# Attention with bias: the last seven head pairs' k and q turned by DMA transposes instead of TensorE

## Chip, cores and metric

One NeuronCore of one Trainium2 chip runs the whole computation in one launch. The metric is the device time of that launch in microseconds (us); the profile's "span" runs from the first to the last instruction of one profiled execution.

## What is computed

Softmax attention with an additive bias that all heads share: 4 x 8 = 32 heads, 1024 positions, head size 64, float32 in and out.

```python
scores = scale * np.matmul(q, k.transpose(0, 1, 3, 2))    # scale = 1/8
scores = scores + bias                                    # (1, 1, 1024, 1024)
attn = np.exp(scores - max) / (np.sum(np.exp(scores - max)) + 1e-8)
return np.matmul(attn, v)
```

## The kernel before

**Tiling.** Heads are taken in 16 pairs (`pr` 0 to 15, even head `t` = 0, odd head `t` = 1). Positions are split as p * 8 + c, with p the partition and c one of 8 chunks. A *slot* is one query chunk of one head: 128 queries against all 1024 keys, 131,072 scores. There are 8 x 32 = 256 slots, in two groups of pairs (9 and 7, `GROUPS`); slots 0 to 143 belong to pairs 0 to 8, slots 144 to 255 to pairs 9 to 15. Every head comes first with three of its chunks, then in the middle of the group with two, then at the end of the group with the other three, so that pair p of the second group is wanted for the first time at slot 144 + 6(p - 9).

**A slot's work.** TensorE fills one of three PSUM places (two banks each) with the scores: 8 matmuls with a chunk of the transposed k as weights and the slot's transposed q as the moving operand (`fill_half`, L277). Bias is added by 8 more matmuls against a scaled identity (L274), but only in a few start slots: afterwards a place is not cleared. The next head's scores come by adding the difference, and for that the operands hold two heads at once. `ko` and `qo` of a pair hold k and q of the even head on partitions 0 to 63 and of the odd head on 64 to 127, the even q negated; `ke` and `qe` hold the even head of this pair and the odd head of the pair before, the odd q negated; `qz` and `qs` hold one head beside zeros for the start slots. Then an exponential turns the place into a bfloat16 tile E: on ScalarE one activation over 1024 columns (`exp`, L291), or, for the slots listed in `PLAN`, on VectorE in five instructions (`d_steps`: `fixed` L308, `frac` L314, `square` L319, `cube` L322, `last` L325), of which only `fixed` reads the place. TensorE multiplies E with v (`av`, L342; v carries a column of ones, so the row sums come along), into banks of up to 7 slots in `ps_x`, which VectorE divides out (`evac`, reciprocal L370 and product L372) and SP's queue stores.

**How k and q come to be.** GpSimd's queue loads them with a cast to bfloat16 into the pool `land`. For pairs 0 to 6 they land as rows, the two heads one behind the other (L156, L168); for pairs 7 to 15 (`BESIDE`) each load is cut in two and lands with the two heads side by side in each chunk (`beside`, L146). TensorE turns a pair's chunk by a transpose into a PSUM tile `px` of the pool `ps_x` (`transposes`, L214), the same two tags that `av` uses. VectorE copies it out to `ko` (L226) or, with the sign, to `qo` (L228). From pair 9 on (`EARLY`) the other arrays are made by copies of half the partitions from SBUF to SBUF on SP's queue (`copy`, L592): `ke` straight from `ko`, and `qe`, `qz`, `qs` from a negated `qo`, which VectorE writes over the landed q (`negate`, L251). k and q arrays stand in a ring of nine tiles (`RING`), so pair p cannot be written before pair p - 9 has been read for the last time. For pairs 3 to 6 VectorE sets landed rows side by side in one tile of the pool `side` (`set_beside`, L245), and TensorE transposes from there. v of pairs 0 to 6 lands as rows and is moved into `vall` by VectorE (L545); v of pairs 7 to 15 (`INPLACE`) lands there directly, in two loads (L187).

**The order.** Every engine executes its own list in the order in which it was written, and so does every DMA queue's issuer. That order comes from a planner that runs while the kernel is built: it keeps a clock for each engine, takes at each step the piece of work that can start first by its own constants (`EXP`, `FILL`, `COPY`, `LATER` and so on), and emits it. Waits on the chip are by semaphores that the framework puts in. Thus the constants set the order alone, and the chip's real durations decide who waits in it. `PLAN` lists the slots that VectorE takes.

## Time and profile before

| what | value |
|---|---|
| median of three runs | 226.95 us (226.21 to 228.2) |
| the profiled execution | 227.0 us, its span 225.2 us |
| granted TensorE clock, mean | 0.998 |
| busy: TensorE / ScalarE / VectorE / GpSimd | 218.0 / 215.1 / 200.9 / 94.4 us |
| slots on ScalarE / VectorE | 230 / 26 |
| DMA packets, of them under 512 B | 92,365, of them 76,256 |

Three engines are busy for nine tenths of the span or more, so shares alone don't say which one sets the end. Busy time of a group merges records that overlap; the mean duration of one instruction is that of its record, and records of consecutive instructions overlap by some tens of nanoseconds, so the distance from start to start is a little shorter. In a row of the timeline the first number is the start in us, the second the length of the merged stretch, and the bracket the idle time before it and who ended it.

### The profile page before, as it was taken

The numbers are of one execution on the slowest core, as the hardware profiler recorded it, in microseconds if no ns is written. First come the engines' busy times: TensorE is split into PE (matmuls) and PEld (weight loads), VectorE is DVE, ScalarE is ACT, GpSimd is POOL, SyncE is SP. The second block draws the span as 40 slices with busy tenths as digits, with TensorE's granted clock in tenths as the row PEclk, the third lists the DMA queues.
The fourth block names the chain that finished last, engine by engine and source line by source line (L and its number), as shares of the span: only waits on it lengthen the run. The fifth ranks groups of instructions, "written<-read, shape, count | busy, mean of one in ns | idle before, by whom it ended". The sixth has DMA issues, their size and how long they took to land.

```text
span 225.2 us, 10472 instructions
## 1 busy us (share of the span) xinstructions
PE 218.0 (97%) x4535; PEld 208.2 (92%) x4535; DVE 200.9 (89%) x311; ACT 215.1 (95%) x235; POOL 94.4 (42%) x160
## 2 busy tenths in 40 slices
PE   7999999999999999999999999999999999999994
PEld 2779989999999999999999999999999999999993
DVE  3587888999999999799999999999999999999853
ACT  3799999999999999999999999999999999999993
POOL 8816577767575875307457475661000000000000
PEclk9999999999999999999999999999999999999999
DMA  5999999999999999498999999989111111112123
GB/s 194 218 204 216 225 211 172 169 202 173 131 129 155 112 142 109 60 209 111 200 165 195 182 141 201 119 107 88 45 44 45 44 44 45 44 37 50 44 60 100
DMA packets 92365, 28.95 MB, mean 129 GB/s; under 512 B 76256, under 2 KB 89056, under 8 KB 92320
## 3 DMA queue, kind: packets, MB, share of 16 engines
q0 software_dynamic: 62880, 14.06, 69.2%
q1 hardware_dynamic: 29008, 13.61, 24.1%
q8 instruction: 35, 0.57, 1.1%
q10 hardware_dynamic: 432, 0.62, 0.9%
q14 instruction: 10, 0.08, 0.1%
HBM read 29.36 MB, written 8.39 MB: 168 GB/s over the span
## 4 chain that ended last, share of the span: by engine, by line
PE 57%; ACT 13%; DMA 11%; DVE 10%; issue 6%; SPq 0%; DVEq 0%; ACTq 0%
PE pl L277 32%; PE po L342 17%; ACT E L291 13%; DMA out_dram<-ob 9%; PE px L214 5%; PE pl L274 2%; DMA dy<-in_q_dram 2%; DVE ob L372 2%; DVE dy L308 1%; DVE df L322 1%; DVE ko L226 1%; DVE df L319 1%; PE px L218 1%; DVE qe L239 1%; DVE qo L228 1%
## 5 line engine op out<-in xcount | busy, mean ns | idle before, releaser
L291 ACT ACTIVATE E<-pl 128x1024 bf16<-128x1024 f32 (+1 forms) x231 | 211.9, 1094 | 2.4 <-PE pl L277 2.2
L342 PE MATMUL po<-vall,E 128*128 128x65 bf16 x1840 | 87.3, 194 | 0.7 <-DVE ob L372 0.4
L277 PE MATMUL pl<-qo,ko 128*128 128x128 bf16 x1024 | 76.1, 219 | 0.6 <-ACT E L291 0.2
L342 PEld LDWEIGHTS <-E 128*128 128x128 bf16 x1840 | 74.3, 98 | 1.6 <-DVE ob L372 0.6
L277 PEld LDWEIGHTS <-ko 128*128 128x128 bf16 x1160 | 69.1, 98 | 2.3 <-issue 0.7
L277 PE MATMUL pl<-qe,ke 128*128 128x128 bf16 x888 | 66.7, 219 | 0.6 <-ACT E L291 0.2
L277 PEld LDWEIGHTS <-ke 128*128 128x128 bf16 x888 | 53.5, 98 | 2.8 <-issue 0.3
L308 DVE TENSOR_SCALAR dy<-pl 128x1024 int32<-128x1024 f32 x26 | 31.7, 1220 | 1.3 <-PE pl L277 0.5
L322 DVE SCALAR_TENSOR_TENSOR df<-de,df 128x1024 f32<-128x1024 f16 x26 | 31.6, 1217 | 0.1
L325 DVE SCALAR_TENSOR_TENSOR de<-dy,df 128x1024 uint16<-128x1024 int32 x26 | 31.6, 1217 | 0.1
L372 DVE TENSOR_TENSOR ob<-po,rs 128x448 f32<-128x448 f32 (+4 forms) x40 | 23.3, 583 | 1.4
L146 POOL DMA_DIRECT2D q<-in_q_dram x18 | 16.0, 891 | 9.6 <-DVE q L251 6.6
L146 POOL DMA_DIRECT2D k<-in_k_dram x18 | 16.0, 890 | 8.2 <-PE px L214 5.5
L187 POOL DMA_DIRECT2D vall<-in_v_dram x18 | 16.3, 907 | 6.9 <-PE po L342 4.8
L314 DVE TENSOR_SCALAR de<-dy 128x1024 f16<-128x1024 uint16 x26 | 19.0, 733 | 0.0
L319 DVE TENSOR_TENSOR df<-de 128x1024 f16<-128x1024 f16 x26 | 17.7, 683 | 0.1
L226 DVE COPY ko<-px 128x1024 bf16<-128x1024 bf16 (+1 forms) x16 | 10.7, 666 | 3.5 <-PE px L218 2.2
L228 DVE TENSOR_SCALAR qo<-px,sgn 128x1024 bf16<-128x1024 bf16 (+2 forms) x18 | 12.3, 686 | 0.5 <-PE px L214 0.2
L370 DVE RECIPROCAL rs<-po 128x7 f32<-128x7 f32 (+5 forms) x41 | 8.0, 194 | 5.0 <-PE po L342 4.4
L516 POOL COPY tick<-vall 1x1 bf16<-1x1 bf16 x14 | 9.0, 643 | 6.1 <-DMA vall<-in_v_dram 5.8
L274 PE MATMUL pl<-ident,braw 128*128 128x128 bf16 x136 | 11.5, 227 | 0.0
L342 PE MATMUL po<-vall,de 128*128 128x65 bf16 x208 | 11.0, 194 | 0.0
(63 smaller groups left out, 141.1 us busy)
## 6 DMA issues: line engine op xcount, KB each, us to landing
out_dram<-ob SPq DMA_DIRECT2D x74, 64.0 KB, 2.9
ke<-ko SPq DMA_DIRECT2D x20, 128.0 KB, 4.7
out_dram<-ob SPq DMA_DIRECT2D x24, 96.0 KB, 3.7
k<-in_k_dram POOLq DMA_DIRECT2D x18, 128.0 KB, 4.8
q<-in_q_dram POOLq DMA_DIRECT2D x18, 128.0 KB, 4.7
vall<-in_v_dram POOLq DMA_DIRECT2D x18, 128.0 KB, 5.1
braw<-in_bias_dram POOLq DMA_DIRECT2D x7, 256.0 KB, 5.4
v<-in_v_dram POOLq DMA_DIRECT2D x7, 256.0 KB, 6.7
```

What stands on the lines that cost most here:

```text
L146: nc.gpsimd.dma_start(out=t[:, :, y, :], in_=(qf, kf)[x][pr][:, y].rearrange("p (c d) -> p c d", d=D))
L187: nc.gpsimd.dma_start(out=vall[:, (2 * pr + t) % VR, :, :D], in_=vf[pr][:, t])
L274: nc.tensor.matmul(to, braw[:, c, :].rearrange("p (kp kc) -> p kc kp", kc=NCH)[:, kc, :], ident8[:], start=i == 0, stop=False, skip_group_ ...
L277: nc.tensor.matmul(to, kk[:, kc, :], qq[:, c, :], start=False, stop=True, skip_group_check=True)
L291: nc.scalar.activation(e[:, i:i + n].rearrange("p b x -> p (b x)"), places[slots[s][0]][:, i:i + n].rearrange("p b x -> p (b x)"), ACTF.Ex ...
L308: w.tensor_scalar(t["y"][:], places[slots[s][0]].rearrange("p b x -> p (b x)"), scale * LOG2E * 65536.0, 128.0 * 65536.0, op0=ALU.mult, op ...
L314: w.tensor_scalar(t["f"], t["lo"], CA / 65536.0, CA * CR, op0=ALU.mult, op1=ALU.add)
L319: w.tensor_tensor(t["s"], t["f"], t["f"], op=ALU.mult)
L322: w.scalar_tensor_tensor(t["w"][:], t["f"], -CC, t["s"], op0=ALU.add, op1=ALU.mult)
L325: w.scalar_tensor_tensor(etile[s].bitcast(U16).rearrange("p c q -> p (c q)"), t["y"][:], 1.0 / 512.0, t["w"][:], op0=ALU.mult, op1=ALU.add)
L342: nc.tensor.matmul(po[:, j + i, :], etile[s][:, kc, :], vall[:, slots[s][2] % VR, kc, :], start=j + i + kc == 0, stop=kc == NCH - 1, skip_ ...
L372: nc.vector.tensor_tensor(ob[:, :n, :], po[:, :n, :D], rs[:, :n, :].to_broadcast([P, n, D]), op=ALU.mult)
```

## The change

For pairs 9 to 15 k and q now land as rows, in one load each. VectorE sets the two heads of k side by side in a tile of the pool `side` (L594), and those of q with the sign in two instructions (L597). SP's queue then issues a DMA transpose from that tile straight into `ko` or `qo` (`turn_over`, L570): 14 transposes of 128 x 1024 bfloat16, 256 KB each, which replace 112 transposes on TensorE and 14 copies out of PSUM on VectorE. The negation of `qo` and the copies on SP's queue stay; the negated q is written over the side tile. `next_turn` lets at most four side tiles be held (`SIDES`), a k tile until its transpose has landed, a q tile until the last copy from it has. To make room `land` has three tiles of each name instead of four, and one `qz` serves both groups of pairs. `INPLACE` shrinks with `BESIDE`, so that v of pairs 9 to 15 lands as rows and is moved by VectorE (L548). VectorE gets 27 slots instead of 26, at other places. The seven numbers of `DUE` change too, but they time TensorE transposes of pairs 9 to 15, of which there are none left.

```diff
-    LANDS = 4
+    LANDS = 3
-    SIDE, SIDES, SIDEND = 3, 1, 9
+    SIDE, SIDES, SIDEND = 3, 4, 9
-    qz = [consts.tile([P, NCH, P], BF, name=f"qz{x}") for x in range(2)]
+    qz = consts.tile([P, NCH, P], BF)
-    PLAN = (34, 42, 55, 63, 74, 80, 84, 99, 107, 112, 122, 125, 137, 141, 157, 164, 174, 178, 179, 196, 200,
-            208, 219, 225, 229, 243)
+    PLAN = (34, 42, 57, 60, 67, 83, 89, 93, 96, 110, 115, 134, 141, 145, 151, 155, 171, 178, 187, 193, 198,
+            204, 206, 222, 232, 237, 243)
-    BESIDE = {0: range(7, NP), 1: range(7, NP)}
-    INPLACE = range(7, NP)
+    BESIDE = {0: range(7, 9), 1: range(7, 9)}
+    INPLACE = range(7, 9)
+    XBAR = range(9, NP)
...
-        nc.gpsimd.memset(qz[0][D:, :, :], 0.0)
+        nc.gpsimd.memset(qz[D:, :, :], 0.0)
-        nc.vector.memset(qz[1][D:, :, :], 0.0)
...
+        xbar = [x[:2] for x in pieces if x[0] in XBAR]
+        pieces = [x for x in pieces if x[0] not in XBAR]
...
+        TURN, TURNED, SIDED, held = 7200, 2200, (640, 430), {}
...
+        def turn_over(pr, which, t):
+            nonlocal t_sp, t_dma
+            name = ("qo", "ko")[which]
+            nc.sync.dma_start(out=arrays(pr)[name][:], in_=raws[pr, which, 0].rearrange("p c t d -> p (c t d)"),
+                              transpose=True)
+            t_sp += 850
+            t_dma = max(t_dma, t) + TURNED
+            done = t + TURN
+            ready[("ko", pr) if which else ("qo", pr, 0)] = done
+            if which:
+                held[pr, 1] = done
+            doubles(pr, which, 0, NCH, done, False)
+
+        def next_turn():
+            while xbar and sum(x > t_dve for x in held.values()) < SIDES:
+                pr, which = xbar[0]
+                ring = max(last_slot.get(pr - RING, -1), last_of.get(2 * (pr + 1 - RING), -1) if linked(pr) else -1)
+                r = raw_at.get((pr, which, 0))
+                if r is None or ring >= next_fill:
+                    return
+                xbar.pop(0)
+                held[pr, which] = 1e12
+                cost = SIDED[which]
+
+                def run(t, pr=pr, which=which, cost=cost):
+                    x = side.tile([P, NCH, 2, D], BF, name="side")
+                    if which:
+                        nc.vector.tensor_copy(x.rearrange("p c t d -> p t c d"), lands[pr, which, 0][:])
+                    else:
+                        for i, sign in ((0, -1.0), (1, 1.0)):
+                            nc.vector.tensor_scalar(x[:, :, i], lands[pr, which, 0][:, i], sign, 1.0, op0=ALU.mult,
+                                                    op1=ALU.mult)
+                        freed(pr, t)
+                    raws[pr, which, 0] = x
+                    sp_q.append((t + cost + L_DVE, lambda t3: turn_over(pr, which, t3)))
+                dve_q.append((r, 2, cost, run))
...
-                freed(pr, ready[key])
+                if pr in XBAR:
+                    held[pr, 0] = ready[key]
+                else:
+                    freed(pr, ready[key])
```

How the lists of the engines change, at two places. First VectorE where pairs 9 and 10 are prepared, after the last slot of pair 0 has been read (`px` is the PSUM tile of a TensorE transpose, `ob` a finished bank of outputs, `dy`, `df` and `de` the tiles of the five-step exponential, `side` a side tile, `k16` and `q16` landed rows). Before, these twelve rows stand in a row:

```order
L226 COPY ko_2523<-px_2502 128x1024
L308 TENSOR_SCALAR dy_2544<-pl0_109 128x1024
L228 TENSOR_SCALAR qo_2568<-px_2547,sgn_98 128x1024
L251 TENSOR_SCALAR q16_894<-qo_2568 128x1024
L314 TENSOR_SCALAR de_2597<-dy_2544 128x1024
L319 TENSOR_TENSOR df_2620<-de_2597 128x1024
L226 COPY ko_2652<-px_2622 128x1024
L370 RECIPROCAL rs_2672<-po_2474 128x7
L372 TENSOR_TENSOR ob_2674<-po_2474,rs_2672 128x448
L308 TENSOR_SCALAR dy_2698<-pl2_111 128x1024
L228 TENSOR_SCALAR qo_2730<-px_2710,sgn_98 128x1024
L251 TENSOR_SCALAR q16_1056<-qo_2730 128x1024
```

There the negation (L251) stands right behind the copy that it reads. Now the side tiles of pair 9's k and q are set at this point, those of pair 10 four rows later, and the negations come further on in VectorE's list, behind other work; from pair 9's q (`side_2504`) to its negation:

```order
L597 TENSOR_SCALAR side_2504<-q16_1043 128x8x64 x2
L315 TENSOR_SCALAR de_2531<-dy_2401 128x1024
L315 TENSOR_SCALAR de_2561<-dy_2448 128x1024
L320 TENSOR_TENSOR df_2573<-de_2531 128x1024
L594 COPY side_2593<-k16_1170 128x2x8x64
L597 TENSOR_SCALAR side_2613<-q16_1173 128x8x64 x2
L371 RECIPROCAL rs_2643<-po_2468 128x7
L373 TENSOR_TENSOR ob_2645<-po_2468,rs_2643 128x448
L320 TENSOR_TENSOR df_2663<-de_2561 128x1024
L323 SCALAR_TENSOR_TENSOR df_2573<-de_2531,df_2573 128x1024
L371 RECIPROCAL rs_2725<-po_2622 128x6
L373 TENSOR_TENSOR ob_2727<-po_2622,rs_2725 128x384
```

Behind these twelve come `cube` of another slot and one `fixed`, then pair 9's negation, pair 11's side tiles, another `fixed` and pair 10's negation:

```order
L323 SCALAR_TENSOR_TENSOR df_2663<-de_2561,df_2663 128x1024
L309 TENSOR_SCALAR dy_2786<-pl2_110 128x1024
L252 TENSOR_SCALAR side_2504<-qo_2591 128x1024
L594 COPY side_2820<-k16_1322 128x2x8x64
L371 RECIPROCAL rs_2833<-po_2715 128x6
L373 TENSOR_TENSOR ob_2835<-po_2715,rs_2833 128x384
L597 TENSOR_SCALAR side_2858<-q16_1325 128x8x64 x2
L309 TENSOR_SCALAR dy_2886<-pl1_109 128x1024
L252 TENSOR_SCALAR side_2613<-qo_2675 128x1024
```

So the copies out of PSUM are gone, and VectorE reaches a negation, which reads what a DMA transpose has written, after about ten other instructions. Second, SP's queue at the same place of the program. Before, the stores of one bank are followed by pair 9's copies and the first of pair 10's:

```order
L592 DMA ke_1330<-ko_2523 64x1024
L592 DMA ke_2556<-ko_2523 64x1024
L592 DMA qe_1399<-q16_894 64x1024
L592 DMA qe_2618<-q16_894 64x1024
L592 DMA qz1_102<-q16_894 64x1024
L592 DMA ke_2556<-ko_2652 64x1024
L592 DMA ke_2685<-ko_2652 64x1024
```

Now four transposes and the stores of two more banks go ahead of them:

```order
L570 DMA_TRANSPOSE ko_2543<-side_2499 128x8x128
L570 DMA_TRANSPOSE qo_2591<-side_2504 128x8x128
L570 DMA_TRANSPOSE ko_2631<-side_2593 128x8x128
L570 DMA_TRANSPOSE qo_2675<-side_2613 128x8x128
L810 DMA out_0_dram<-ob_2645 128x2x64
L810 DMA out_0_dram<-ob_2645 128x128
L810 DMA out_0_dram<-ob_2645 128x2x64
L810 DMA out_0_dram<-ob_2645 128x64
L810 DMA out_0_dram<-ob_2727 128x2x64 x2
L810 DMA out_0_dram<-ob_2727 128x64 x2
L632 DMA ke_1310<-ko_2543 64x1024
L632 DMA ke_2818<-ko_2543 64x1024
```

The copies moved behind the transposes and behind eight stores. The last pair's last copy (`qe` of pair 15) stood in SP's list behind the stores of the bank that completes 131 slots and now stands behind those of the bank that completes 159; in TensorE's list 149 slots have been filled before that bank's products, and now 168, while pair 15 is first read when 179 and now 178 have been. TensorE's list itself loses the 112 transposes, and in it the products with v follow the fills more closely: at slot 136 the fills are 17 slots ahead of the products before, and 4 now.

More of the change, by code (lines that the diff above doesn't have):

```diff
@@ L201, in arrays @@
             if pr in first_pair:
-                t["qz"] = qz[group_of[pr] % 2]
+                t["qz"] = qz
             arrs[pr] = t
@@ L451 @@
         pieces += [y for x in zip(k_items[n1:], q_items[n1 + SPLIT:]) for y in x]
+        xbar = [x[:2] for x in pieces if x[0] in XBAR]
+        pieces = [x for x in pieces if x[0] not in XBAR]
         due = {p: d for p, d in zip(range(EARLY, NP), DUE)}
         need_at = {}
-        for p, which, c0, n in pieces:
+        for p, which, c0, n in pieces + [(*x, 0, NCH) for x in xbar]:
             need_at[p, which, c0] = min(s for s, x in enumerate(slots) if x[2] // 2 == p and (c0 == 0 or x[1] >= c0))
@@ L632, in next_side @@
         def next_side():
-            if side_q and len(side_open) < SIDES and side_q[0] in raw_at:
+            if side_q and len(side_open) < 1 and side_q[0] in raw_at:
                 pr, which, c0 = side_q.pop(0)
@@ L859 @@
         while next_fill < NS or next_act < len(acts) or avq or dav or dve_q or sp_q:
+            next_turn()
             c = []
```

2 lines of the change are left out of this document (1 added, 1 removed).

## Prediction

> **What bounds the kernel now.** I read the page first, for the shares, and then ScalarE's timeline, because three engines are nearly full and only a timeline tells which of them never waits.
>
> ```profile
> span 225.2 us, 10472 instructions
> PE 218.0 (97%) x4535; PEld 208.2 (92%) x4535; DVE 200.9 (89%) x311; ACT 215.1 (95%) x235; POOL 94.4 (42%) x160
> ```
> ```profile
> 9.06 31.14 ACT L291 ACTIVATE E<-pl 128x512 bf16<-128x512 f32 x34 [0.47 <-PE pl L277]
> 40.70 18.44 ACT L291 ACTIVATE E<-pl 128x1024 bf16<-128x1024 f32 x20 [0.50 <-PE pl L277]
> 59.38 67.31 ACT L291 ACTIVATE E<-pl 128x1024 bf16<-128x1024 f32 x73 [0.24 <-PE pl L277]
> 126.99 94.58 ACT L291 ACTIVATE E<-pl 128x1024 bf16<-128x1024 f32 x103 [0.30 <-PE pl L277]
> 222.06 0.34 ACTq L767 DMA_DIRECT2D out_dram<-ob  x1
> ```
>
> The reader is to see four stretches of exponentials without a gap, one after the other, from 9.06 to 126.99 + 94.58 = 221.57 us, with 0.47 + 0.50 + 0.24 + 0.30 = 1.5 us of idle time before them, all ended by TensorE's fills. In the last stretch one exponential takes 94.58 / 103 = 0.918 us. At that price the other three should last 33 x 0.918 + 0.6 (one of the 34 is half a slot) = 30.9, 18.4 and 67.0 us; they last 31.14, 18.44 and 67.31, so 0.6 us more of waiting hides in them. ScalarE's list of 230 slots is therefore the bound, about 2.1 us of it are waits, and the rest of the 225.2 us is about 8 us ahead of the first exponential and 3.6 us behind the last. TensorE, busier by the page, waits for ScalarE as often as the other way round; what it is relieved of shows only in those 2.1 us.
>
> The profiled execution took 227.0 us, 1.8 more than its span and within 0.05 of the median of 226.95, so I work from 227.0 and need no correction.
>
> **The change, part by part.** The prices on VectorE and TensorE:
>
> ```profile
> L308 DVE TENSOR_SCALAR dy<-pl 128x1024 int32<-128x1024 f32 x26 | 31.7, 1220 | 1.3 <-PE pl L277 0.5 <-ACT E L291 0.4
> L325 DVE SCALAR_TENSOR_TENSOR de<-dy,df 128x1024 uint16<-128x1024 int32 x26 | 31.6, 1217 | 0.1
> L322 DVE SCALAR_TENSOR_TENSOR df<-de,df 128x1024 f32<-128x1024 f16 x26 | 31.6, 1217 | 0.1
> L314 DVE TENSOR_SCALAR de<-dy 128x1024 f16<-128x1024 uint16 x26 | 19.0, 733 | 0.0
> L319 DVE TENSOR_TENSOR df<-de 128x1024 f16<-128x1024 f16 x26 | 17.7, 683 | 0.1
> L372 DVE TENSOR_TENSOR ob<-po,rs 128x448 f32<-128x448 f32 x27 | 16.9, 624 | 0.9
> L370 DVE RECIPROCAL rs<-po 128x7 f32<-128x7 f32 x27 | 5.4, 200 | 2.0 <-PE po L342 1.8
> L228 DVE TENSOR_SCALAR qo<-px,sgn 128x1024 bf16<-128x1024 bf16 x14 | 10.4, 746 | 0.4 <-PE px L214 0.2
> L226 DVE COPY ko<-px 128x1024 bf16<-128x1024 bf16 x15 | 10.2, 682 | 3.4 <-PE px L218 2.2 <-PE px L214 1.2
> L239 DVE TENSOR_SCALAR qe<-qo 64x384 bf16<-64x384 bf16 x3 | 1.1, 350 | 0.0
> L251 DVE TENSOR_SCALAR q<-qo 128x1024 bf16<-128x1024 bf16 x7 | 3.7, 533 | 0.6
> L545 DVE COPY vall<-v 128x1024 bf16<-128x1024 bf16 x7 | 3.3, 471 | 0.1
> L245 DVE COPY side<-q 128x1024 bf16<-128x1024 bf16 x4 | 2.4, 594 | 3.2 <-PE px L214 3.2
> L245 DVE COPY side<-k 128x1024 bf16<-128x1024 bf16 x4 | 1.7, 431 | 0.3 <-PE px L214 0.3
> ```
> ```profile
> 92.37 0.45 PE px L214 x8
> ```
> ```profile
> 20.00:210.00 190.00, 188.08 (x4010) 183.65 (x4008) 180.48 (x264) 188.81 (x206) 81.53 (x136) 1.00 1.00 125
> 92.00:156.00 64.00, 63.60 (x1371) 62.51 (x1369) 61.07 (x86) 63.58 (x70) 34.56 (x51) 1.00 1.25 155
> ```
>
> *One slot more on VectorE.* ScalarE runs 229 slots instead of 230: -0.92 us on the path that sets the end.
>
> *112 TensorE transposes less.* The chain of waits prices eight of them at 0.45 us, so 14 x 0.45 = 6.3 us of TensorE go, all between about 92 and 140 us, where it is busy for 63.6 of 64. This doesn't shorten ScalarE's list; it can remove ScalarE's waits in that part, the 0.30 at 126.99 and the 0.3 hidden in the stretch before. The waits earlier than 59 us, 1.5 of the 2.1, stay, since loads and lists are the same there but for one fill of zeros that VectorE drops. I take half of the 0.6: -0.3, with 0 and -0.6 as ends.
>
> *VectorE's load.* Gone are 7 x 0.682 + 7 x 0.746 = 10.0 us of copies out of PSUM. Added are 7 side tiles of k at 0.43 to 0.59 (I take 0.43, the row of the same operand), 7 of q as two half-size multiplications (nearest row 0.35 for 384 columns; 0.35 to 0.5 each, I take 0.35, so 4.9 in all), 7 moves of v at 0.47, and one slot of 1.220 + 1.217 + 1.217 + 0.733 + 0.683 = 5.07. That is 3.0 + 4.9 + 3.3 + 5.1 = 16.3, net +6.3 us by records (up to 9.5 with the upper ends). Between 20 and 210 us VectorE is idle for 190 - 180.5 = 9.5 us, so it still fits beneath ScalarE, but with 3 us left, or nothing. In itself this costs 0; without that cover the excess would appear as late `fixed` steps, each of which holds one of three places.
>
> *The DMA transposes.* Nothing in the trace is a transpose. The nearest rows:
>
> ```profile
> ke<-ko SPq DMA_DIRECT2D x20, 128.0 KB, 4.7
> qe<-q SPq DMA_DIRECT2D x13, 128.0 KB, 4.2
> k<-in_k_dram POOLq DMA_DIRECT2D x6, 256.0 KB, 6.9
> ```
> ```profile
> 94.99 1.12 SPq L592 DMA_DIRECT2D ke<-ko  x2
> 128.64 3.04 SPq L767 DMA_DIRECT2D out_dram<-ob  x3
> 138.34 0.47 SPq L592 DMA_DIRECT2D qe<-q  x1
> ```
>
> From 4.2 (a copy of half the bytes) to 9.4 us (two copies of 4.7 end to end); I take 6.9, the row with the same bytes. What hides it is VectorE's list: between pair 9's side tile of q and its negation stand two `frac`, two `square`, two `cube`, one `fixed`, two side tiles and two evacuations: 2 x 0.733 + 2 x 0.683 + 2 x 1.217 + 1.220 + 1.13 + 2 x 0.82 = 9.3 us by records. Starts follow each other more closely than records last, by some 7% (an estimate: over 92 to 160 us the groups' busy times add up to 70 us where VectorE as a whole was busy for 65), so 8.6 us. The transpose is issued behind that of k, 0.56 us later by the copies' row, and would land at 0.56 + 6.9 = 7.5: hidden, with 1 us to spare. At 9.4 VectorE would wait about 1.4 us. For pair 10's q, the fourth transpose of a burst, the list from pair 9's side tile of k to that negation holds 0.7 + 9.3 + 0.533 + 0.43 + 0.82 + 0.7 + 1.220 = 13.7 us by records, 12.7 from start to start; if the four pass one behind the other, they may take (12.7 - 0.56) / 4 = 3.0 us each. Cost by the value taken: 0; by the upper end, see the second rival.
>
> *SP's queue and the wait it adds.* Copies cost SP 0.56 us each, stores up to 3.04 / 3 = 1.0. Fourteen issues at 0.56 to 1.0 are 8 to 14 us more between 92 and 156 us. What is queued behind a transpose are stores and the copies that make `ke` and `qe`; who waits for these is TensorE's fill of the next pair. Pair 15's last copy was issued at 138.34 and is wanted at slot 180, the 161st of ScalarE's list before, whose exponential starts at about 126.99 + 34 x 0.918 = 158 us, its fill 2 us earlier: 17 us of cover. In the new lists that copy stands ten fills ahead of the first use, some 8 us, less 4.2 for its landing. The cover shrinks to about 4 us and is not used up. Cost 0.
>
> *Loads.* k, q and v of seven pairs come in one load each instead of two; GpSimd issues 21 fewer. Three landing tiles instead of four start pair 12's load only when pair 9's q has been set aside, and in VectorE's list those rows are read after the 13 us up to pair 10's negation and 4 more (two `last`, a `frac`, an evacuation), against 6.9 for the landing. The one `qz` left is free once slot 92 is filled, and pair 9's copy into it stands behind the stores of 97 finished slots. Cost 0.
>
> Sum: 227.0 - 0.92 - 0.3 = 225.8 us. Ends: -0.6 from the waits and 0 to +2 for a VectorE with nothing left give 225.5 to 228.
>
> The Trainium skill's page "DMA: Bandwidth & Descriptors", section "Latency and other measured facts", gives DMA transposes an effective 261 GB/s; 256 KB would then pass in about 1.0 us, an estimate, and the forecast would hold with room. The page "VectorE: DVE Perf Modes", section "The three transpose paths", speaks against the change: 1309 ns for 128 x 128 by DMA against 390 by TensorE; eight such blocks one after the other would be 10.5 us, an estimate, and the sum would be that of the third rival. No run here has shown either yet.
>
> **The rivals.** *Everything goes:* also the early waits vanish, 227.0 - 0.92 - 2.1 = 224.0. Against it: three quarters of them lie where nothing changes. Chance 0.08.
>
> *VectorE stands at the negations.* If a transpose lands in 9.4 us instead of 6.9, each of seven negations holds VectorE for about 1.4 us, and behind it wait side tiles, evacuations and `fixed` steps: 10 us, of which 3 are idle anyway, 7 to make up. A single wait is under the 2 x 0.918 us that two other filled places give ScalarE; the sum isn't. If between half and all of the 7 us reach the end, 227.0 - 0.9 + 3.5 to 7 = 229.6 to 233, the middle 231.4. It decides from about 8 us of landing, or 3.0 us each in a burst of four. For it: DMA rows of this stretch are slow, VectorE is full, and four transposes come at once. Against: 6.9 us for the same bytes out of DRAM. Chance 0.27.
>
> *Transposes one after another.* If each holds the stream for its whole 6.9 us, 14 take 97 us, from 92 to 189; with the copies the last pair is there at about 194 instead of 156, and the fixed order makes ScalarE wait for it: 227 - 0.9 + 38 = 264. It decides from (156 - 5 - 92) / 14 = 4.2 us each. For it: nothing in the trace shows how such a transfer spreads over the 16 engines. Against: the copies beside it do overlap, two issued 0.56 us apart landing 4 us after issue. Chance 0.10.
>
> **How the numbers follow.** Forecast 0.55, the three rivals 0.08, 0.27 and 0.10. One per cent, 2.3 us, is about what a measurement of this kernel can tell from no change. Faster by over 1% (under 224.7) is the first rival and the very edge of the forecast: 0.09. Slower by over 1% (over 229.2) are the second and third, 0.37, less a little of the second that stays below: 0.36. Within 1%: 0.55. The forecast's own range is 224.9 to 228. For eight times in ten I leave out the third rival and a few hundredths at either end: 224.4 to 233.
>
> **What would show it.** Right: ScalarE's timeline has 229 slots in gapless stretches from 92 us on, transposes land within 7 us, negations (L252) show no idle time before them. Second rival: VectorE's idle time before L252 or L597, ended by a transpose, about 1.4 us each, and ScalarE idle behind `fixed`. Third: TensorE waiting for `ko`, `ke` or `qe` past slot 144. If VectorE's list simply runs late without any DMA wait, my load sum was too low. The prediction is wrong if transposes cost SP's queue much more than a copy, or if loads through three landing tiles come late.

## The result, and the profile after

The changed kernel takes 246.22 us, the median of four executions (245.59 to 247.23), beside 226.76 us for the kernel before (four, 226.21 to 228.2): 1.084 times as long, with an interval of 1.081 to 1.088. The prediction was 225.8 us and its range ended at 233.0; the time lies 13 us above that end. The profiled execution after took 245.59 us, 18.6 more than the one before (227.0).

The head of the page after, its busy line and three rows of its 40 slices (6.1 us each):

```profile
span 243.6 us, 10179 instructions
PE 218.7 (90%) x4423; PEld 207.8 (85%) x4423; DVE 201.4 (83%) x331; ACT 215.3 (88%) x234; POOL 62.2 (26%) x118
...
DVE  2497899879999999866257688399989999899994
ACT  3699999989999999999821699869999999999993
PEclk9999999999999999999977799979999999999999
```

Hardly an engine has more work than before: ScalarE is busy for 215.3 us (215.1 before), VectorE for 201.4 (200.9), TensorE for 218.7 (218.0). The 18.6 us are waits, all but a fraction, and the slices show where: ScalarE's row falls to 2, 1 and 6 at slices 20 to 22, which is 122 to 140 us, and once more to 6 near 160; VectorE's row thins out earlier, from slice 16 on. ScalarE's timeline has the size of the gaps (start, length, operation, and in brackets the idle time before it and who ended it):

```profile
117.84 2.85 ACT L292 ACTIVATE E<-pl 128x1024 bf16<-128x1024 f32 x3
125.86 1.02 ACT L292 ACTIVATE E<-pl 128x1024 bf16<-128x1024 f32 x1 [5.17 <-PE pl L278]
...
134.53 1.02 ACT L292 ACTIVATE E<-pl 128x1024 bf16<-128x1024 f32 x1 [5.44 <-PE pl L278]
...
138.20 19.36 ACT L292 ACTIVATE E<-pl 128x1024 bf16<-128x1024 f32 x21 [1.36 <-PE pl L278]
160.64 3.77 ACT L292 ACTIVATE E<-pl 128x1024 bf16<-128x1024 f32 x4 [3.08 <-PE pl L278]
```

Four gaps, 5.17 + 5.44 + 1.36 + 3.08 = 15.05 us, all ended by a fill of TensorE's. In all, ScalarE waits 19.5 us for fills, where it was 2.2. From 164.75 us on the exponentials run as densely as before. Three of the four can be followed back row by row. TensorE's two long waits behind the first two, from its timeline:

```profile
118.80 0.61 PE L278 MATMUL pl<-qe,ke 128*128 128x128 bf16 x8
124.29 0.62 PE L343 MATMUL po<-vall,E 128*128 128x65 bf16 x8 [4.88 <-DVE ob L373]
124.72 1.04 PE L278 MATMUL pl<-qo,ko 128*128 128x128 bf16 x8
...
132.96 0.62 PE L343 MATMUL po<-vall,de 128*128 128x65 bf16 x8 [4.93 <-DVE de L326]
```

It waits first for an evacuation (`ob`, L373), then for a `last` step (`de`, L326), both VectorE's. VectorE, from its timeline, had stood before them:

```profile
106.61 0.43 DVE L252 TENSOR_SCALAR side<-qo 128x1024 bf16<-128x1024 bf16 x1 [2.19 <-DMA qo<-side]
...
111.78 0.43 DVE L252 TENSOR_SCALAR side<-qo 128x1024 bf16<-128x1024 bf16 x1 [1.99 <-DMA qo<-side]
...
120.59 0.43 DVE L594 COPY side<-k 128x1024 bf16<-128x1024 bf16 x1 [4.74 <-DMA qz<-side]
...
123.61 0.62 DVE L373 TENSOR_TENSOR ob<-po,rs 128x448 f32<-128x448 f32 x1
...
128.70 0.43 DVE L252 TENSOR_SCALAR side<-qo 128x1024 bf16<-128x1024 bf16 x1 [2.63 <-DMA qo<-side]
```

The negations (L252) wait for a transposed q, 10.7 us in four waits over the whole run. The longest single wait is another one: at 120.59 the side tile of a later k (L594) needs one of the four side tiles, and the one that it gets is free only when the copy into `qz` has landed. The evacuation that TensorE wants from 119.4 us on stands three microseconds of work behind it on the same in-order engine. The gap near 160 us has the same shape: a negation at 155.91 waited 3.92 us for a turned q, TensorE then waited 3.02 us for a `last` step behind it, and ScalarE 3.08 us for TensorE. SP's queue shows why that copy is late; a row is one issue or several of a kind, its second number the time that they hold the queue:

```profile
96.51 1.33 SPq L570 DMA_TRANSPOSE ko<-side  x1
97.95 3.29 SPq L570 DMA_TRANSPOSE qo<-side  x1
101.34 1.62 SPq L570 DMA_TRANSPOSE ko<-side  x1
103.08 3.12 SPq L570 DMA_TRANSPOSE qo<-side  x1
106.31 5.81 SPq L810 DMA_DIRECT2D out_dram<-ob  x8
112.16 1.13 SPq L632 DMA_DIRECT2D ke<-ko  x2
...
114.62 0.60 SPq L632 DMA_DIRECT2D qz<-side  x1
```

The four transposes of pairs 9 and 10 hold the queue from 96.51 to 106.2. Eight stores that had come due meanwhile go next, and pair 9's copies follow at 112.16, though its turned k had landed at 103.1 and its negation was done at 107.0. The `qz` copy, issued at 114.62, has landed when VectorE goes on at 120.59. The view of line 570 gives all fourteen transposes (ns: least, median, most, for which one holds the queue):

```profile
L570 SPq DMA_TRANSPOSE ko<-side x7: 1247/1335/2179, 96.5 to 159.9; - x7
L570 SPq DMA_TRANSPOSE qo<-side x7: 1244/2130/3290, 97.9 to 161.3; - x7
...
DMA to landing us min/median/max: 3.5/5.9/9.6
```

The queue's single rows add up to 25.4 us of hold for the fourteen, 1.81 each, three times the 0.56 of a copy. The median landing of 5.9 us hides a difference: those of q, which the negations read, took 7.2 us in the median, and the four that a negation waited for landed 8.64, 8.67, 8.65 and 7.18 us after their issue.

Last, TensorE's clock. The same 20 us of before and of after (busy time of each engine, then the granted clock, DMA share and GB/s), the first row from before:

```profile
120.00:140.00 20.00, 19.95 (x440) 19.68 (x438) 19.59 (x30) 19.70 (x23) 12.46 (x18) 1.00 1.45 177
```
```profile
120.00:140.00 20.00, 10.78 (x175) 10.66 (x176) 13.28 (x24) 7.50 (x8) 3.87 (x7) 0.74 1.19 221
```

The granted clock is 0.74 there and was 1.00; a fill of eight matmuls that took 0.61 us at 118.80 takes 1.04 at 124.72, behind the gap. ScalarE runs 8 exponentials in these 20 us, where it ran 23.

### The profile page after: what moved, and what is told of

It reads as the page before. It is cut to its first block, busy times and chain, and to the rows that moved or that the text cites. A ratio compares the mean times of both kernels' runs of the same rounds, so it can differ in the third digit from the quotient of the medians.

```text
span 243.6 us, 10179 instructions
## 1 busy us (share of the span) xinstructions
PE 218.7 (90%) x4423; PEld 207.8 (85%) x4423; DVE 201.4 (83%) x331; ACT 215.3 (88%) x234; POOL 62.2 (26%) x118
## 4 chain that ended last, share of the span: by engine, by line
PE 35%; ACT 25%; DMA 17%; DVE 10%; issue 8%; SPq 2%; POOL 1%; DVEq 0%; ACTq 0%; POOLq 0%
ACT E L292 25%; PE pl L278 22%; PE po L343 11%; DMA out_dram<-ob 4%; DMA ke<-ko 3%; DMA q<-in_q_dram 3%; DMA qe<-side 3%; DMA v<-in_v_dram 2%; PE pl L275 2%; DMA df<-in_k_dram 2%; DVE dy L309 2%; DVE df L323 2%; DVE de L326 1%; SPq L570 1%; DVE ob L373 1%
## 5 line engine op out<-in xcount | busy, mean ns | idle before, releaser
L292 ACT ACTIVATE E<-pl 128x1024 bf16<-128x1024 f32 (+1 forms) x230 | 212.2, 1091 | 19.6 <-PE pl L278 19.5
L278 PEld LDWEIGHTS <-ko 128*128 128x128 bf16 x1160 | 71.4, 99 | 5.9 <-issue 2.2
L278 PEld LDWEIGHTS <-ke 128*128 128x128 bf16 x888 | 55.0, 99 | 4.4 <-issue 1.9
L326 DVE SCALAR_TENSOR_TENSOR de<-dy,df 128x1024 uint16<-128x1024 int32 x27 | 32.9, 1217 | 0.0
L373 DVE TENSOR_TENSOR ob<-po,rs 128x384 f32<-128x384 f32 (+3 forms) x42 | 23.7, 564 | 1.5
L183 POOL DMA_DIRECT2D v<-in_v_dram x14 | 10.0, 711 | 31.7 <-DVE vall L548 30.3
L343 PEld LDWEIGHTS <-de 128*128 128x128 bf16 x216 | 9.5, 101 | 8.6 <-DVE de L326 8.5
L157 POOL DMA_DIRECT2D k<-in_k_dram x13 | 9.4, 721 | 18.2 <-DVE side L594 14.4
L252 DVE TENSOR_SCALAR side<-qo 128x1024 bf16<-128x1024 bf16 x7 | 3.0, 424 | 10.7 <-DMA qo<-side 10.7
L371 DVE RECIPROCAL rs<-po 128x6 f32<-128x6 f32 (+3 forms) x42 | 8.0, 191 | 3.7 <-PE po L343 3.4
L275 PEld LDWEIGHTS <-braw 128*128 128x128 bf16 x136 | 9.9, 148 | 0.3 <-DMA braw<-in_bias_dram 0.2
L169 POOL DMA_DIRECT2D q<-in_q_dram x13 | 9.3, 713 | 1.3 <-issue 0.7
```

What stands on the lines that cost most here:

```text
L157: nc.gpsimd.dma_start(out=t.rearrange("p t c d -> p t (c d)"), in_=kf[pr])
L183: nc.gpsimd.dma_start(out=lands[pr, "v"].rearrange("p t c d -> p t (c d)"), in_=vf[pr].rearrange("p t c d -> p t (c d)"))
L275: nc.tensor.matmul(to, braw[:, c, :].rearrange("p (kp kc) -> p kc kp", kc=NCH)[:, kc, :], ident8[:], start=i == 0, stop=False, skip_group_ ...
L278: nc.tensor.matmul(to, kk[:, kc, :], qq[:, c, :], start=False, stop=True, skip_group_check=True)
L292: nc.scalar.activation(e[:, i:i + n].rearrange("p b x -> p (b x)"), places[slots[s][0]][:, i:i + n].rearrange("p b x -> p (b x)"), ACTF.Ex ...
L326: w.scalar_tensor_tensor(etile[s].bitcast(U16).rearrange("p c q -> p (c q)"), t["y"][:], 1.0 / 512.0, t["w"][:], op0=ALU.mult, op1=ALU.add)
```

## The experiments

The theory after reading the two traces: a transpose is dear where it is issued, not where it lands. It holds SP's queue, what stands behind it goes out late, and VectorE stands in order for both. The rivals: the slots' new places, the room given up (one of four landing tiles, one of two `qz`), bytes as such, or the late landing alone. All runs are single executions beside one of the kernel before on the same chip; executions of the kernel before ranged from 226.2 to 228.2, so that a ratio below means little beyond one per cent. For orientation, all but the small kernel of the first experiment:

| run | us | before, same chip | ratio |
|---|---|---|---|
| after_plan26 | 245.32 | 226.53 | 1.083 |
| after_k_turned | 243.09 | 226.87 | 1.072 |
| after_stores_pool | 241.05 | 226.53 | 1.064 |
| before_room_turns | 240.17 | 226.53 | 1.060 |
| after_replanned | 238.69 | 226.87 | 1.052 |
| before_room_copies | 234.68 | 226.87 | 1.034 |
| after_plain | 233.89 | 227.33 | 1.029 |
| before_room_blocks | 233.68 | 227.69 | 1.026 |
| after_fewer_stores | 230.85 | 227.33 | 1.016 |
| before_room | 229.62 | 226.53 | 1.014 |
| before_plan27 | 230.20 | 227.33 | 1.013 |

**What a transpose costs by itself.** A kernel of transposes and copies between tiles of SBUF, first one by one beside loads, then with nothing beside them:

```diff
+        for i in range(3):
+            nc.sync.dma_start(out=a[i + 1][:], in_=flat(a[i][:]), transpose=True)
+        for i in range(4):
+            nc.sync.dma_start(out=c[i][:], in_=flat(a[3][:]), transpose=True)
...
+        for i in range(1, 6):
+            nc.sync.dma_start(out=h[i][:64], in_=a[1][:64])
...
+        for i in range(6):
+            nc.sync.dma_start(out=e[i][:], in_=flat(a[3][:]), transpose=True)
```

> Leaves out the whole attention: only DMA transposes of 128 x 1024 bfloat16 from SBUF to SBUF on SP's queue, in four parts: three in a chain, each reading what the one before wrote; four at once with nothing beside them; then five copies of 64 x 1024; then six at once beside twelve loads with a cast on GpSimd's queue. In the changed kernel a transpose held SP's queue for 1.24 to 3.29 us and landed after 3.5 to 9.6. Theory A (a transpose is dear by itself): the hold is at least 1.2 us and a landing at least 3.5 even alone, and in the burst of four the holds grow to 3 us again, with landings spaced by the same 2 to 3 us. Theory B (it is only the company: loads, stores and copies on the same DMA engines): alone the hold falls to the 0.5 us of a copy and the landing to about 2.5, and only the six beside the loads are slow.

Each view of a line closes with the time from issue to landing; first the three one by one beside the loads, then four at once and five plain copies of 128 KB, then the last six transposes, when the loads had ended:

```profile
L31 SPq DMA_TRANSPOSE a<-a x3: 1232/1242/1327, 2.0 to 19.8; - x3
...
DMA to landing us min/median/max: 4.4/6.7/11.2
```
```profile
L33 SPq DMA_TRANSPOSE c<-a x4: 1232/1331/1337, 24.2 to 28.2; - x4
```
```profile
L39 SPq DMA_DIRECT2D h<-a x5: 462/596/603, 34.9 to 37.3; - x5
```
```profile
L47 SPq DMA_TRANSPOSE e<-a x6: 1239/1328/1337, 41.5 to 48.2; - x6
...
DMA to landing us min/median/max: 3.1/3.3/3.4
```

Alone a transpose lands in 3.3 us, sooner than any bound of the prediction, but it holds the queue for 1.33 us, twice a copy. Beside loads the landing goes to 4.4 to 11.2. Theory A thus held for the hold and failed for the landing and for the burst: four at once with nothing beside them stayed at 1.33 us of hold and 3.3 of landing. Theory B's 0.5 us of hold fell. The loads weren't where the last six were to meet them, so that part of the question is answered by the first three only; their hold stayed at 1.23 to 1.33 us beside the loads. Six issues from 41.46 to 48.24 are 1.36 us apart: 256 KB each, 193 GB/s. The Trainium skill's page "DMA: Bandwidth & Descriptors", section "Latency and other measured facts", has an effective 261 GB/s for transposes; a single queue didn't reach it here. Eight blocks of 128 x 128 in 3.3 us also don't bear out an eightfold 1309 ns, which I had made of the Trainium skill's page "VectorE: DVE Perf Modes", section "The three transpose paths".

**Copies in place of the transposes.** The same order, the same bytes, nothing turned:

```diff
-            nc.sync.dma_start(out=arrays(pr)[name][:], in_=raws[pr, which, 0].rearrange("p c t d -> p (c t d)"),
-                              transpose=True)
+            nc.sync.dma_start(out=arrays(pr)[name].rearrange("p c q -> p (c q)"),
+                              in_=raws[pr, which, 0].rearrange("p c t d -> p (c t d)"))
```

> The changed kernel with each DMA transpose replaced by a plain copy of the same 256 KB from the side tile to the same array, so that k and q of pairs 9 to 15 stay unturned; every list keeps its order. Theory A (the price of the transposes, 1.2 to 3.3 us of SP's queue each and 6 to 9 us to land): a copy holds SP for 0.6 us and lands in about 5, VectorE's 10.7 us of standing before the negations fall under 3, ScalarE's idle time under 5 us, and the time comes to 227 to 232 us. Rival (the route itself: two more stages on SP's queue, four side tiles, VectorE's order): ScalarE still idles for more than 12 us and the time stays over 238.

```profile
L570 SPq DMA_DIRECT2D ko<-side x7: 483/540/575, 95.9 to 148.1; - x7
L570 SPq DMA_DIRECT2D qo<-side x7: 484/540/566, 96.5 to 148.8; - x7
...
DMA to landing us min/median/max: 3.1/5.4/7.3
```

233.89 us, between the two expectations: 12 of the 19.5 us are gone. The copies land in 5.4 us in the median where the transposes took 5.9, those of q in 5.6 where it was 7.2; the fourteen hold the queue for 7.4 us in place of 25.4, and no negation waits. So turning, and not moving the same bytes at the same places, is most of the loss. Hold and landing fell together, so this run doesn't tell them apart. What remains, 1.029, is in part the same wait for a side tile as in the change, here 2.75 us for the `qz` copy and 1.77 us for a `qe` copy, with TensorE behind it:

```profile
114.22 0.43 DVE L594 COPY side<-k 128x1024 bf16<-128x1024 bf16 x1 [2.75 <-DMA qz<-side]
...
124.46 0.62 PE L343 MATMUL po<-vall,de 128*128 128x65 bf16 x8 [3.83 <-DVE de L326]
```

ScalarE's two longest gaps from 92 us on, 3.56 us at 126.03 and 1.98 at 130.33, come right behind. The places and the room are taken up below.

**Only k turned.** q's seven are plain copies, k's seven transposes:

```diff
+            if not which:
+                nc.sync.dma_start(out=arrays(pr)[name].rearrange("p c q -> p (c q)"), in_=rows)
+            else:
+                nc.sync.dma_start(out=arrays(pr)[name][:], in_=rows, transpose=True)
```

> The changed kernel with the seven transposes of q replaced by plain copies of 256 KB at the same places; the seven of k stay. Leaves out: q of pairs 9 to 15 is not turned, so their outputs are not the reference's. All 14 turned: 246.2 us; none turned (after_plain): 233.9. Theory A (each transpose adds its own share through queue and DMA engines): in the middle, 238 to 242 us, with SyncE's queue held about 16 us by the 14 in place of 25. Rival B (it is the wait for the turned q at the negation that costs, since VectorE waits for q alone there): q now lands early, so 233 to 236 us and no wait at the negation. Rival C (the first burst of four decides, with two transposes in it as good as none): 234 to 237 us, but with waits at the negation of about 2 us.

243.09 us, above all three expectations: with half of the transposes, three quarters of the price are back (9.2 of the 12.3 us between after_plain and the change). The views of the two lines say why:

```profile
L574 SPq DMA_TRANSPOSE ko<-side x7: 1248/1345/4132, 96.4 to 157.3; - x7
```
```profile
L572 SPq DMA_DIRECT2D qo<-side x7: 488/505/1336, 97.8 to 158.7; - x7
...
  DVE side L252: 8.2, 3
...
DMA to landing us min/median/max: 3.5/6.2/8.5
```

The second transpose of the burst still holds the queue for 4.13 us, and the plain copies of q that stand behind transposes land late and are waited for, 8.2 us at the negations, where after_plain had no such wait. VectorE waits 4.81 us for the `qz` copy as well. The price isn't halved with the number of transposes, as Theory A had it; which of the seven bring most of it isn't shown, since the waits at the negations are spread from 106 to 153 us.

**The stores.** The stores of banks finished from the 86th to the 165th slot are left out; then, in a second kernel, they go through GpSimd's queue:

```diff
+                    skip = 84 < len(av_done) < 166
-                    sp_q.append((t2 + cost + L_DVE, lambda t3, to=to, of_=of_, w=w: w.dma_start(out=to, in_=of_), end))
+                    sp_q.append((t2 + cost + L_DVE, lambda t3, to=to, of_=of_, w=w, skip=skip: skip or w.dma_start(out=to, in_=of_), end))
```
```diff
-                    w = nc.scalar if end else nc.sync
+                    w = nc.scalar if end else nc.gpsimd if 84 < len(av_done) < 166 else nc.sync
```

> The changed kernel without the stores of the banks that are finished when 85 to 165 slots have been multiplied with v, so that this part of the output is left out; the other instructions keep their order. Rival B (SP's queue is too full: some 45 stores at 0.45 us among the transposes and copies hold these up): 20 us of SP's time are freed between 92 and 165, ScalarE's idle time falls under 6 us and the time to 226 to 232. Theory A: the transposes still hold SP and land late, the first four as before; the time falls by 2 to 6 us, to 240 to 244.

> The changed kernel with the stores of the banks finished when 85 to 165 slots have been multiplied with v issued by GpSimd's queue instead of SP's; nothing is left out, and TensorE's, VectorE's and ScalarE's lists are the same. Theory (SP's queue is the stage that is too full: 65 us of issue in the 78 us from 92 to 170, 25 of them transposes): SP is relieved of some 20 us as in the run without these stores, and the time comes to 230 to 235 us. Rival (there it was the DMA engines and HBM that were relieved, not the queue): the bytes still move, so the time stays at 241 us or more.

Without the stores it is 230.85 us, in the rival's range; the 240 to 244 us of my theory fell. SP's queue in that run, from the first to the last of the same four transposes and on to the `qz` copy:

```profile
93.73 1.33 SPq L570 DMA_TRANSPOSE ko<-side  x1
...
99.65 2.55 SPq L570 DMA_TRANSPOSE qo<-side  x1
102.30 2.04 SPq L632 DMA_DIRECT2D ke<-ko  x2
...
105.79 0.60 SPq L632 DMA_DIRECT2D qz<-side  x1
```

The transposes are no cheaper: they hold the queue for 29.4 us in all, where it was 25.4, with single holds of up to 3.9 us, and land in 7.5 us in the median. But pair 9's copies follow at once. The `qz` copy goes out 105.79 - 93.73 = 12.1 us behind the burst's first issue, where it was 18.1, and VectorE's one wait for it, 4.74 us in the change, is down to 0.5. So hold and landing of the transposes don't make the loss by themselves; with the stores gone from the queue, and their bytes with them, most of it went. Moving the stores to another queue gave only 5.2 us of it (241.05, the rival's value, where I had expected 230 to 235): there one evacuation waited 6.2 us for a store of its buffer to land, a wait that came with the move, and the transposes, with the same bytes beside them, held SP for 32.5 us in all, up to 4.5 at a time. That points to a cost of the stores through the DMA engines as well as through the queue; the two runs don't divide it.

**The places of the 27 slots, both ways.** Before with after's list, and after with before's:

```diff
-    PLAN = (34, 42, 55, 63, 74, 80, 84, 99, 107, 112, 122, 125, 137, 141, 157, 164, 174, 178, 179, 196, 200,
-            208, 219, 225, 229, 243)
+    PLAN = (34, 42, 57, 60, 67, 83, 89, 93, 96, 110, 115, 134, 141, 145, 151, 155, 171, 178, 187, 193, 198,
+            204, 206, 222, 232, 237, 243)
```

> The kernel before with the 27 VectorE slots of the changed kernel and nothing else; the planner orders around them. Theory A (the transposes are the cause): VectorE has 5 us more work and its slots lie at places chosen for other work, so 227 to 232 us. Rival C (the slots at these places are what makes VectorE late): most of the loss is here too, over 236 us.

> The changed kernel with the 26 VectorE slots of the kernel before; the planner orders around them. Theory (SP's queue is too full with the transposes): SP's load is the same, so 238 us or more. Rival C (27 slots at the new places overload VectorE): 232 us or less.

Before gets 2.9 us slower with 27 slots, though ScalarE has 0.92 us less to do; after stays where it was with 26 (245.32). Both are as my theories expected (227 to 232, and 238 or more). The run on the kernel before changes number and places together, so its 2.9 us aren't the price of the slot alone. With the old list the change keeps its loss, so the places aren't its cause.

**The room, and transposes that nobody waits for.** Before with three landing tiles and one `qz`; the same with a transpose of a spare tile at the fourteen places where a k or q has been copied out; with a plain copy of 256 KB there; and with a transpose of one block of 128 x 128:

```diff
-    LANDS = 4
+    LANDS = 3
-    qz = [consts.tile([P, NCH, P], BF, name=f"qz{x}") for x in range(2)]
+    qz = consts.tile([P, NCH, P], BF)
```
```diff
+                                if pr >= EARLY:
+                                    turned.append(pr)
+                                    nc.sync.dma_start(out=spare[len(turned) % 2][:], transpose=True,
+                                                      in_=spare[2].rearrange("p c q -> p (c q)"))
```

> The kernel before with the room of the change alone: three landing tiles instead of four, one array qz for both groups of pairs. Theory: the loads of the late pairs have cover, so within 2 us of before, 226 to 229 us. Rival D (landing with three tiles is what comes late): over 235 us.

> The kernel of before_room with 14 DMA transposes of 256 KB added to SP's queue, one behind each copy out of PSUM of pairs 9 to 15, from a constant tile to spare tiles that nobody reads. The added cost alone, without side tiles, and with nobody waiting for a transpose. Theory (the transposes hold SP's queue, and this hurts because VectorE and TensorE wait for what stands behind them): each holds SP for 1.2 us or more, 20 to 28 us in all, the copies behind them are late, but the first use of each pair is some 17 us away, so 0 to 5 us over before_room. Rival E (transposes slow every other transfer on the DMA engines so much that loads and stores come late everywhere): more than 8 us over before_room.

> The control for before_room_turns: the kernel before with the changed kernel's room (three landing tiles, one qz) and, at the same 14 places of SyncE's queue, a plain copy of 256 KB from one spare tile to another in place of each spare transpose. Nobody waits for them. before_room took 229.6 us, before_room_turns 240.2. Theory A (the price is the transpose's own: it holds SyncE's queue for 1.2 to 3.3 us and its many small pieces fill the DMA engines): a plain copy holds the queue for about 0.5 us, so 230 to 233 us, ScalarE idle under 7 us. Rival B (any 14 further transfers of 256 KB would do it, by their bytes): 237 to 241 us, ScalarE idle 11 to 15 us, and the loads land as late as beside the transposes (5.6 us the landed k of 128 KB instead of 4.8).

> before_room_turns with each of the 14 spare transposes cut to one block of 128x128, an eighth of its bytes, at the same places of SyncE's queue and with the same waits. before_room took 229.6 us, with 14 plain copies of 256 KB 234.7, with 14 transposes of 256 KB 240.2. Theory A (the price goes with the bytes and pieces that the DMA engines carry, and the long holds of the queue follow from them): 229 to 232 us, each hold under 0.7 us, and ScalarE idle under 6 us. Rival B (the price goes with the number of DMAs on the queue, their issue and the wait of each for the one eight back): 234 to 238 us, with ScalarE idle 8 to 13 us though hardly any bytes are moved.

The room alone costs 3.1 us (1.014), little more than single runs can tell and a little over the 226 to 229 that I had expected; ScalarE waits 4.6 us for fills, in nine small waits, where it was 2.2. Fourteen transposes that no instruction reads add 10.6 us to that; my theory had 0 to 5, the rival more than 8. The three views, transposes, copies, blocks:

```profile
L744 SPq DMA_TRANSPOSE spare<-spare x14: 1231/1315/3267, 93.0 to 159.2; - x14
...
DMA to landing us min/median/max: 5.0/6.6/7.5
```
```profile
L744 SPq DMA_DIRECT2D spare<-spare x14: 484/598/1680, 92.9 to 150.1; - x14
...
DMA to landing us min/median/max: 3.8/5.0/7.0
```
```profile
L744 SPq DMA_TRANSPOSE spare<-spare x14: 1093/1234/2141, 93.9 to 155.9; - x14
```

By ratios, room 1.014, blocks 1.026, copies 1.034, transposes 1.060. Theory and rival for the copies both missed: 234.7 us lies between 230 to 233 and 237 to 241, and so does the blocks' 233.7 between 229 to 232 and 234 to 238. A block with an eighth of the bytes holds the queue as long as a whole transpose, 1.23 us for 1.32, against my "under 0.7": the hold goes with the instruction. So the price seems to have two parts: the blocks, with few bytes and 19.1 us of hold in all, cost 1.2% over the room alone; the copies, with all the bytes and 12.8 us of hold, 2.0%; whole transposes, with the bytes and 23.1 us, 4.6%. With one execution each and a spread of about one per cent these sizes are rough, and neither variant has one part alone. The Trainium skill's page "Advanced Engine Details and Errata", section "X-Bar Transpose (TRN2)", holds transposes to be as fast as regular DMAs; at the same places they held the queue 2.2 times as long in the median, landed in 6.6 us for 5.0, and cost 5.5 us more.

How something that nobody waits for comes to cost time shows on TensorE, in the run with spare transposes:

```profile
125.00 0.61 PE L216 MATMUL px<-ident,q 128*128 128x128 bf16 x8 [2.15 <-DMA q<-in_q_dram]
...
135.32 1.01 PE L216 MATMUL px<-ident,k 128*128 128x128 bf16 x8 [2.21 <-DMA k<-in_k_dram]
```

Here and once more by 2.1 us at 141 TensorE waits for loads, which it did nowhere in this stretch of before_room. They are on GpSimd's queue, not on SP's; loads of k of 128 KB land in 5.6 us there and in 4.8 without the transposes. Part of the price is company on the DMA engines.

**An order that allows for them.** Four planning numbers set nearer to what was measured, and a list of 27 places that fits:

```diff
-        TURN, TURNED, SIDED, held = 7200, 2200, (640, 430), {}
+        TURN, TURNED, SIDED, held = 8000, 2200, (640, 430), {}
-            t_sp += 850
+            t_sp += 1300
+            landed.append(t + TURN)
...
-                c.append((max(t_sp, o[0]), 3))
+                c.append((max(t_sp, o[0], landed[-8] if len(landed) > 7 else 0), 3))
```

> The changed kernel with four numbers of its planner set nearer to what was measured (a transpose lands after 8.0 us in place of 7.2 and holds SyncE's queue for 1.3 us in place of 0.85, a copy takes 5.0 us, and a DMA of SyncE's queue waits for the one eight back) and another list of 27 places for VectorE's exponentials that fits these; the work is the same. By the planner's own clock the list is 7.7 us longer than the changed kernel's was by its own. Theory A (the order of the work doesn't allow for the transposes' time, and an order that does hides most of it): 231 to 237 us, with less than 4 us of waits for turned q. Rival B (queue and DMA engines are loaded by the transposes wherever they stand): 241 to 248 us, with SyncE's queue as full between 92 and 145 us as it was (46 of 53 us) and ScalarE idle over 14 us.

```profile
L570 SPq DMA_TRANSPOSE ko<-side x7: 1240/1305/2083, 94.5 to 155.1; - x7
L570 SPq DMA_TRANSPOSE qo<-side x7: 1231/1800/2927, 96.3 to 158.5; - x7
...
  DVE side L252: 2.6, 1
```

238.69 us, between the two expectations. An order that knows the price takes the wait for turned q from 10.7 us to 2.6 and wins 7.5 of the 19.5 us. SP's queue is as full as it was (45 of 53 us between 92 and 145, by the sum of its rows; 46 in the change), and ScalarE still waits 12.6 us for fills. Order and list together give back two fifths, the load stays. No version with transposes beat the kernel before.

## Why the prediction was wrong

**The step that failed** is SP's queue: "Fourteen issues at 0.56 to 1.0 are 8 to 14 us more", "The cover shrinks to about 4 us and is not used up. Cost 0." I priced a transpose's issue by the rows of copies and stores. Measured are 25.4 us, 1.33 each when alone and up to 3.3 in the burst. The hold alone isn't the loss: at 29.4 us of it the run without stores took 230.85 us. Its consequences were in no term. What stands behind on the queue goes out late: pair 9's copies of k 9.1 us after the turned k had landed, those from the negated q 6.4 us (pair 9) and 10.1 us (pair 10) after the negation. A side tile is held until those have landed, and VectorE stands for that tile with TensorE's evacuation behind it. I asked who waits for the copies, answered "TensorE's fill of the next pair", and overlooked that the change itself had made VectorE a second one, through the four side tiles. The sentence on what would make it wrong named the cause.

**The landing** of 6.9 us was near the median of all (5.9, 3.5 to 9.6), but too short where it counted: 8.64, 8.67, 8.65 and 7.18 us for the four that a negation waited for, and for the first two of these 3.3 and 3.1 us were hold. So "hidden, with 1 us to spare" failed as well: I gave the four of a burst 3.0 us each from start to start; from the first issue at 96.51 to the end of VectorE's wait at 111.78 they took 15.3, 3.8 each.

**The second rival** (0.27) had the right place and side and too small a price, 231.4 us at the middle: seven waits of 1.4 us at the negations. There were four of 2.0 to 3.9 us, 10.7 together; that the sum came out near is luck, as neither their number nor their length was as assumed. What it lacked are the side tiles (5.1 us at L594), and that two of these waits came close together, so that three engines stood one behind the other and TensorE's clock fell as well. I had counted a wait on VectorE as at most its own length at the end; here 16.6 us of such waits between 92 and 172 us (the sum of its DMA-ended idle times) stand against 15.05 in ScalarE's long gaps. For the 4.74, the 2.63 and the 3.92 us the rows show the way to a gap; for the rest only the sums agree.

**Transposes one after another** didn't happen: fourteen passed in 65 us amid other traffic, and TensorE waited for no `ko`, `ke` or `qe` from a DMA.

**One slot more on VectorE**, -0.92: the slot moved, but before_plan27, with other places as well, shows a loss of 2.9 us where a gain was forecast. **The 112 TensorE transposes less**: its busy time rose by 0.7 us all the same, in part since the rest took longer at a granted clock of 0.74 (120 to 140 us) and 0.93 (140 to 165). **Loads and room**, "Cost 0": before_room shows 3.1 us for them, another mis-sized term; three landing tiles and one `qz` weren't tried apart. **VectorE's load**, +6.3 us by records, came out at +2.8 (217.4 for 214.6) and wasn't at fault: its busy time rose by 0.5, and it stood idle for 6.7 of the 20 us from 120 to 140.

Two smaller points were off without weight for the sum: TensorE doesn't wait for ScalarE "as often as the other way round" (two waits of its matmuls, 0.3 us, against five of ScalarE, 2.2 us), and the forecast's range is given once from 225.5 and once from 224.9.

What stays open: why a hold grows from 1.33 us to 3 or 4 in company, since loads beside single transposes didn't do it and the run without stores still had holds of 3.9; and how the price divides between hold, landing and the DMA engines in the changed kernel itself. No run gave VectorE more side tiles, or set the copies ahead of the stores.

## What to carry to other kernels

A DMA that takes work off a busy engine is priced three times: at its issue on the queue, in its bytes beside other traffic, and in what stands behind it on that queue; a price for its issue has to come from an instruction of the same kind. Before an in-order engine is made to wait for a DMA's result or for a buffer that a DMA releases, list what that engine owes to others behind the wait, since such a wait can be handed on nearly whole: 3.92 us of VectorE came out as 3.08 of ScalarE. Small transfers that others need may be worth a place ahead of stores, which can wait; no run here has tried that order by itself.

## What the hardware showed beside that

A transpose held the issuing queue for 1.23 us even for one block of 128 x 128, and for 1.33 with eight; the bytes show in the landing (2.2 us at best for one block in before_room_blocks, 3.3 for eight in turns_alone) and not in the hold. A plain copy queued behind transposes was slowed with them: 8.46 us to land, issued at 97.83 in after_k_turned, where the same copy took 6.54 in after_plain. And the granted clock of TensorE fell to 0.74 in the 20 us with two gaps of 4.9 us, was 1.00 from 140 to 160 us, 0.66 in the 5 us behind a gap of 3.0, and 1.00 from 165 us on. Eight matmuls behind a gap took 1.04 us in place of 0.61, so that a wait cost more than its length.
